# The front of a diffusion-transformer layer: who makes the low parts, in which order the first two projection blocks are multiplied, and when the masks are loaded

## The chip, the cores and the metric

The kernel runs on one core of a Trainium2 chip. The metric is the device time of one execution in microseconds, the median of several runs of the same program. Before the change it is 1540.49 us (three runs, 1539.71 to 1542.42). One execution was also recorded by the hardware profiler; all rows of the profile come from that one.

The core has five engines that run side by side, each with its own queue: TensorE (PE, matrix products; PEld is its weight load), VectorE (DVE), ScalarE (ACT), GpSimd (POOL), and SyncE (SP), which here only issues transfers. ScalarE issues a few transfers too.

## The reference

One layer of a hybrid backbone over 1024 latent tokens and 256 context tokens, width 1024, float32. Both kinds of token get their own adaLN vectors (shift and scale) from `SiLU(c) @ w_ada + b_ada`. What the front of the kernel computes is the first lines of this:

```python
mod_x = (jax.nn.silu(c) @ w_ada[i] + b_ada[i])[:, None, :]
mod_c = jax.nn.silu(c_ctx) @ w_ada[i] + b_ada[i]
px = modulate(rms_norm(x, norm1_w[i]), sh1, sc1) @ w_in[i]
pc = modulate(rms_norm(ctx, norm1_w[i]), csh1, csc1) @ w_in[i]
```

with `rms_norm(x, w) = x * rsqrt(mean(x*x) + eps) * w` and `modulate(h, shift, scale) = h * (1 + scale) + shift`. The columns of `w_in` feed a gated DeltaNet (short convolution, forward and backward scans) and a 2-D neighbourhood attention. Both results are concatenated and projected, and a SwiGLU feed-forward follows.

## The kernel before

**Layout.** Tokens lie along the free axis: 256 context tokens, then 1024 latent ones, 1280 in all. The width 1024 is cut into eight tiles of 128 partitions (`KT = 8`), called k below. A projection block is 128 output columns for all 1280 tokens; its sum over the eight tiles stands in three banks of the accumulation memory, for columns 0 to 256, 256 to 768 and 768 to 1280 (`SEGS`).

**Split products.** A float32 product is made of three faster ones. Every operand is split into a high part, rounded to the fast matmul type, and a low part, the rest. The terms are: 0, high weight by high tile; 1, high weight by low tile; 2, low weight by high tile. One term of one block and one tile is a group of three matmuls (256, 512 and 512 columns). The names are `whi`/`wlo` (from `fraw`) for the weights of the first two blocks, `zhi`/`zlo` for those of the third, and `hh[k]`/`hl[k]` for the tiles.

**The front, in program order** (lines 625 to 765):

1. The constants `cst` and the masks (256 KB) are loaded from ScalarE's queue. SP loads the eight x tiles, the raw weights of the first block, then eight 1 MB pieces of the adaLN weights (`wada`, seven buffers) with the raw weights of the second block among them. GpSimd casts the masks into `mr`, which is used far later.
2. `sums`: ScalarE squares each x tile, VectorE adds two of them, TensorE multiplies with a matrix of ones. This gives the sum of squares of each token, on all partitions. The first block's weights are split here: high part on ScalarE (line 216), low part on GpSimd (line 217).
3. ScalarE turns the sums into `rs`, the inverse root, by a logarithm and an exponential.
4. `ada(q)`, q = 0 to 3, yields the shift and scale of tiles 2q and 2q+1. It has two halves. In the first, eight products of `wada` leave a row, copied out of the bank by VectorE (q = 0, 1) or ScalarE. In the second, eight tiny products turn the row into columns (`pm<-sel,arow`), and VectorE makes `mod1` and `w1s` of them (lines 674, 675).
5. `normed(k)`: VectorE scales a tile in place by `w1s` and `rs` (line 695), first the 256 context columns, then the 1024 latent ones. ScalarE adds the shift and rounds: `hh[k]` (line 696). VectorE makes `hl[k]` (line 698).
6. `products(k, term, n)`: a group of three matmuls for tile k and block n.

`tile_pair` writes the order for tiles 0 and 1, 4 and 5, 6 and 7: terms 0 and 2 of both blocks for the first tile, then those of the second with the two halves of an `ada` between them, and term 1 of both tiles and blocks last. Tiles 2 and 3 are written out in the same manner. The second block's weights are split after `normed(0)`.

**What sets the order.** `pe.pinned` keeps TensorE in exactly the program's order in this stage. All other engines and SP's queue are put in order by a planner: it simulates the program with its own costs and gives each engine, among the instructions it holds to be ready, the one that comes first in the program. Every engine then works through its queue strictly in that order. Buffers are reused as soon as their last reader is done; the front's tiles give their room to later stages, the `wad` buffers of the second modulation (line 230) among them.

**What follows.** The two blocks are taken out of their banks (line 434), VectorE runs the convolution taps over them (line 443), and the other blocks, the scans, the attention and the feed-forward follow. Between the blocks, the second modulation (`modulation`, lines 220 to 257) sums 32 loads of 256 KB on VectorE; it must end (line 238 writes `modp`) before the accumulation banks are shared out anew, near 151 us.

Of the kernel before, what the change touches and what calls it, by code (L numbers as in the profile page):

```python
# [9 lines left out]
F32 = mybir.dt.float32  # L10
# [4 lines left out]
OP = mybir.AluOpType  # L15
# [4 lines left out]
D, L, CT, T = 1024, 1024, 256, 1280  # L20
KT = 8
# [66 lines left out]
def hybrid(ctx, tc, a, dbg):  # L88
    nc = tc.nc
    act, dve, pool, sp = nc.scalar, nc.vector, nc.gpsimd, nc.sync  # L90
# [45 lines left out]
    cst = const("cst", [128, NCONST])  # L136
# [64 lines left out]
            dve.scalar_tensor_tensor(r, y, 1.5, r, op0=OP.add, op1=OP.mult)  # L201

    def weights(wp, raws=2):
        def load(src, kt=KT, n=128, lo_engine=pool, raw=None, keep=None):
# [11 lines left out]
            act.copy(h, r)  # L216
            lo_engine.tensor_tensor(o, r, h.bitcast(F32), OP.subtract)
            return h, o
        return load

# [151 lines left out]
    with ExitStack() as bs:  # L372
# [31 lines left out]
        class Block:  # L404
# [7 lines left out]
            def prefetch(self, raw=None, keep=None):  # L412
# [3 lines left out]
                self.w = load_w(src, raw=raw, keep=keep)  # L416

            def banks(self):
                self.pss = [(bank("blk"), s0, n) for s0, n in self.segs]
# [206 lines left out]
        with ExitStack() as xs:  # L626
            xp = pools(xs, "xp", "left")
            xt = []
            act.dma_start(cst, a["cst"])
            masks = xp.tile([128, 4, 128], F32, name="masks", tag="masks")  # L630
            act.dma_start(masks, a["masks"])
            ascope = ExitStack()
            wap = pools(ascope, "wap", "right", 7)
            aw = {}
# [23 lines left out]
            def ada(q):  # L658

                p = bank("pm")  # L660
                for j in (2 * q, 2 * q + 1):
                    w = aw.pop(j)
                    for k in range(4):
                        pe.matmul(p[32 * k:32 * k + 32], wide[:, 4 * (j % 2) + k], w[:, k], start=j % 2 == 0,
                                  stop=j % 2 == 1)
                row = xp.tile([128, 512], F32, name="arow", tag="arow", bufs=2)
                (act.copy if q > 1 else dve.tensor_copy)(row, p)
                yield
                p = bank("pm")
                for b in range(4):  # L670
                    pe.matmul(p[:, 2 * b:2 * b + 2], row[:, b * 128:(b + 1) * 128], sel, start=True, stop=True)
                col = lambda x, b: x[:, b:b + 2].rearrange("p (b c) -> p b c", c=1).to_broadcast([128, 2, 2])
                for b0, s in ((8 + 2 * q, p[:, 0:4]), (2 * q, p[:, 4:8])):
                    dve.tensor_tensor(mod1[:, b0:b0 + 2], s.rearrange("p (b c) -> p b c", c=2), col(bada, b0), OP.add)
                dve.scalar_tensor_tensor(w1s[:, 2 * q:2 * q + 2], mod1[:, 8 + 2 * q:10 + 2 * q], 1.0, col(n1w, 2 * q),
                                         op0=OP.add, op1=OP.mult)
                yield

            def sums(ps, k):

                for k in (k, k + 1):
                    sq = xp.tile([128, T], F32, name="sq", tag="sq", bufs=4)
                    act.activation(sq, xt[k], AF.Square)
                    if k % 2 == 0:
                        even = sq
                dve.tensor_tensor(sq, sq, even, OP.add)
# [3 lines left out]
            def normed(k):  # L690

                t = xt[k]
                parts = [(1, slice(0, CT)), (0, slice(CT, T))]
                for j, x in parts:
                    dve.scalar_tensor_tensor(t[:, x], t[:, x], w1s[:, k, j:j + 1], rs[:, x], op0=OP.mult, op1=OP.mult)
                    act.activation(hh[k][:, x], t[:, x], AF.Identity, bias=mod1[:, k, j:j + 1])  # L696
                for j, x in parts:
# [12 lines left out]
            for k in (2, 4, 6):  # L710
                sums(ps, k)
            for p, (s0, n) in zip(ps, SEGS):
                act.activation(rs[:, s0:s0 + n], p[:, :n], AF.Ln, bias=b_eps, scale=1.0 / D)
# [10 lines left out]
            def tile_pair(k, nxt):  # L724

                if k:
                    normed(k)
                for term, n in (0, 0), (2, 0), (0, 1), (2, 1):
                    products(k, term, n)
                normed(k + 1)  # L730
                products(k + 1, 0, 0)
                products(k + 1, 0, 1)
                if nxt:
                    next(nxt)
                products(k + 1, 2, 0)
                if nxt:
                    next(nxt)
                products(k + 1, 2, 1)
                for i in (k, k + 1):
                    for n in range(2):  # L740
                        products(i, 1, n)

            tile_pair(0, adas[1])
            normed(2)
            products(2, 0, 0)
            products(2, 0, 1)
            next(adas[2])
            products(2, 2, 0)
            products(2, 2, 1)
            next(adas[2])  # L750
            normed(3)
            products(3, 0, 0)
            products(3, 0, 1)
            next(adas[3])
            products(3, 2, 0)
            next(adas[3])
            products(3, 2, 1)
            ascope.close()
            h_tiles(pools(bs, "hp2", "right"), 4)
            for i in (2, 3):  # L760
                for n in range(2):
                    products(i, 1, n)
            tile_pair(4, None)
            tile_pair(6, None)
            pe.pinned = False

        cp = pools(bs, "cp", "right")
# [584 lines left out]
    class Stream:  # L1352
# [430 lines left out]
```

## Time and profile before

| | us |
|---|---|
| median of three runs | 1540.49 |
| profiled execution, its own time | 1542.52 |
| its span in the trace | 1540.70 |
| TensorE busy | 1467.2 (95%) |
| VectorE busy | 1000.6 (65%) |
| ScalarE busy | 715.1 (46%) |
| GpSimd busy | 188.5 (12%) |

The span runs from the first to the last instruction of the record; the execution's own time is 1.82 us longer. Busy time of TensorE is modelled, since its products are pipelined: a TensorE that is busy may still run at a lowered clock, and the granted clock has a column of its own (1.00 is full speed, 0.50 is half). A row of the order of time has start, duration, engine, line, operation, output and inputs, shape and count; several instructions of one kind may be merged in it. Idle time in brackets is that of the engine ahead of the row, with what released it. A line can be that of a helper: L98 is every matmul.

### The profile page before, as it was taken

How to read it: one execution, taken by the hardware profiler on the slowest of the kernel's cores; microseconds unless marked ns; L12 is line 12 of the kernel's file. 1: busy time of each engine (PE TensorE's matmuls, PEld its weight loads, DVE VectorE, ACT ScalarE, POOL GpSimd, SP SyncE). 2: the span in 40 equal slices, each digit the busy share in tenths (PEclk: the TensorE clock that was granted, in tenths of full speed). 3: DMA queues.
4: the chain of work that ended last, by engine and by line, in shares of the span. 5: the costliest groups of instructions: out<-in, count | busy, mean ns of one | idle time of the engine just before them, and what ended most of it. 6: DMA issues, size and time to landing. Idle time of an engine off the chain costs nothing.

```text
span 1540.7 us, 23901 instructions
## 1 busy us (share of the span) xinstructions
PE 1467.2 (95%) x8553; PEld 1220.9 (79%) x8553; DVE 1000.6 (65%) x1911; ACT 715.1 (46%) x1396; POOL 188.5 (12%) x255
## 2 busy tenths in 40 slices
PE   4999998999999989998898989999999999999998
PEld 2789787778988868887787878888888888888887
DVE  4786579355255657678976489755565656689652
ACT  5343363684375355666643284333333334455441
POOL 1044610343143200000100000000000000000000
PEclk8999999899999999999999999999999999999999
DMA  9277133655477599997529404433332334798742
GB/s 367 95 227 247 47 90 117 234 145 190 151 247 241 157 275 287 276 261 217 171 78 324 149 35 136 147 106 104 105 106 99 106 101 156 237 378 293 235 154 82
DMA packets 208295, 276.30 MB, mean 179 GB/s; under 512 B 15968, under 2 KB 114864, under 8 KB 207152
## 3 DMA queue, kind: packets, MB, share of 16 engines
q1 hardware_dynamic: 207312, 274.15, 55.3%
q8 instruction: 67, 1.10, 0.3%
q10 hardware_dynamic: 864, 0.63, 0.1%
q14 instruction: 52, 0.43, 0.1%
HBM read 209.93 MB, written 68.98 MB: 181 GB/s over the span
## 4 chain that ended last, share of the span: by engine, by line
PE 49%; DVE 2%; ACT 1%; DMA 0%; issue 0%; SPq 0%; ACTq 0%; DVEq 0%
PE ps L98 46%; PE sc L98 2%; PE sc L102 1%; DMA wraw<-w_out 0%; DVE x L1541 0%; DVE bt L316 0%; ACT pt L329 0%; DVE lB L1535 0%; ACT x L1542 0%; DVE s L1227 0%; ACT L1445 0%; DVE bt L321 0%; DVE x L1454 0%; DVE oacc L1249 0%; DVE gal L1258 0%
## 5 line engine op out<-in xcount | busy, mean ns | idle before, releaser
L98 PE MATMUL ps<-hT,uhi 128*128 128x512 f32 x496 | 147.7, 392 | 3.2 <-ACT hT L1534 3.1
L98 PE MATMUL ps<-lT,uhi 128*128 128x512 f32 x496 | 146.7, 390 | 0.0
L98 PE MATMUL ps<-hT,ulo 128*128 128x512 f32 x496 | 146.7, 390 | 0.0
L98 PE MATMUL ps<-hB,uhi 128*128 128x512 f32 x436 | 129.7, 391 | 0.0
L98 PE MATMUL ps<-hB,ulo 128*128 128x512 f32 x436 | 129.3, 390 | 0.0
L98 PE MATMUL ps<-lB,uhi 128*128 128x512 f32 x436 | 129.3, 390 | 0.0
L1410 ACT CAST uhi<-ws 128x512 fp32r<-128x512 f32 x91 | 54.8, 623 | 149.9 <-PE ps L98 89.0
L1410 ACT CAST uhi<-wq 128x512 fp32r<-128x512 f32 x101 | 60.6, 621 | 136.5 <-PE ps L98 71.1
L98 PE MATMUL blk<-hh,whi 128*128 128x512 f32 (+1 forms) x392 | 117.5, 397 | 5.6 <-ACT hh L696 5.2
L1411 DVE TENSOR_TENSOR ulo<-wq,uhi 128x512 fp32r<-128x512 f32 x101 | 67.5, 687 | 69.2 <-ACT uhi L1410 37.5
L98 PEld LDWEIGHTS ps<-hT,uhi 128*128 128x128 f32 x496 | 93.4, 189 | 23.3 <-ACT hT L1534 3.5
L98 PE MATMUL blk<-hh,wlo 128*128 128x512 f32 (+1 forms) x392 | 109.2, 377 | 0.0
L98 PEld LDWEIGHTS ps<-hT,ulo 128*128 128x128 f32 x496 | 93.4, 188 | 19.6
L98 PEld LDWEIGHTS ps<-lT,uhi 128*128 128x128 f32 x496 | 93.4, 188 | 19.5
L98 PE MATMUL blk<-hl,whi 128*128 128x512 f32 (+1 forms) x392 | 106.9, 373 | 0.0
L98 PEld LDWEIGHTS ps<-hB,uhi 128*128 128x128 f32 x436 | 82.3, 189 | 17.5 <-issue 0.5
L98 PEld LDWEIGHTS ps<-hB,ulo 128*128 128x128 f32 x436 | 82.1, 188 | 17.2
L98 PEld LDWEIGHTS ps<-lB,uhi 128*128 128x128 f32 x436 | 82.1, 188 | 17.1
L98 PE MATMUL blk<-zhi,hh 128*128 128x264 f32 (+1 forms) x288 | 84.4, 293 | 1.6 <-DVE cacc L443 1.6
L1411 DVE TENSOR_TENSOR ulo<-ws,uhi 128x512 fp32r<-128x512 f32 x91 | 60.8, 686 | 36.8 <-ACT uhi L1410 28.5
L98 PE MATMUL blk<-zhi,hl 128*128 128x264 f32 (+1 forms) x288 | 81.7, 284 | 0.0
L98 PE MATMUL blk<-zlo,hh 128*128 128x264 f32 (+1 forms) x288 | 81.6, 283 | 0.0
(328 smaller groups left out, 3192.6 us busy)
## 6 DMA issues: line engine op xcount, KB each, us to landing
wq<-w_fo SPq DMA_DIRECT2D x99, 256.0 KB
wq<-w_gu SPq DMA_DIRECT2D x88, 256.0 KB
wad<-wa SPq DMA_DIRECT2D x64, 256.0 KB
bt<-rpb SPq DMA_DIRECT2D x64, 192.0 KB
t_d<-g SPq DMA_DIRECT2D x22, 512.0 KB
fr<-t_d SPq DMA_DIRECT2D x44, 256.0 KB
f_d<-g SPq DMA_DIRECT2D x33, 256.0 KB
fr<-f_d SPq DMA_DIRECT2D x33, 256.0 KB
```

Of the source, the lines that this page charges most:

```text
L98: i = nc.tensor.matmul(*args, **kw)
L102: i = nc.tensor.transpose(*args, **kw)
L1410: act.copy(hi, self.raw[key])
L1411: dve.tensor_tensor(lo, self.raw[key], hi.bitcast(F32), OP.subtract)
```

## The change

- The first block's low part (line 217) is made by VectorE instead of GpSimd, and its split is written behind all four `sums` instead of behind the first.
- The second block's high part is made before the first `ada`; its low part becomes a step `split` of its own on VectorE, behind the scaling of tiles 0 and 1.
- `normed(k)` is cut into `high(k)` (scaling and `hh`) and `low(k)` (`hl`). For tile 0, `high` works in three pieces of 256, 512 and 512 columns instead of two of 256 and 1024.
- The order of steps is written as one list, `plan`. In it `low` comes later than before, and term 1 of a tile comes behind the products of the next one.
- `warm(1)` is called twice: one 512-column product of constants into a bank that nobody reads, once behind the first half of `ada(0)` and once behind its second half.
- The masks' load moves from ScalarE's queue, ahead of the x tiles, to the end of the list of loads on SP; their tile is placed behind the x tiles.

```diff
-            act.dma_start(masks, a["masks"])
...
+            masks = xp.tile([128, 4, 128], F32, name="masks", tag="masks")
+            sp.dma_start(masks, a["masks"])
...
+            def cuts(k):
+                x = [(1, slice(0, CT)), (0, slice(CT, T))]
+                return x if k else x[:1] + [(0, slice(CT, CT + 512)), (0, slice(CT + 512, T))]
...
+            def warm(n):
+
+                p = bank()
+                for _ in range(n):
+                    pe.matmul(p, ident, cst[:, 0:512], start=True, stop=True)
...
-            sums(ps, 0)
-            first[0].prefetch(raws[0])
-            for k in (2, 4, 6):
+            for k in (0, 2, 4, 6):
                 sums(ps, k)
+            first[0].prefetch(raws[0], lo_engine=dve)
...
+            first[1].prefetch(raws[1], later=True)
             adas = [ada(q) for q in range(4)]
             next(adas[0])
+            warm(1)
             next(adas[0])
-            normed(0)
-            first[1].prefetch(raws[1])
+            warm(1)
             for b in first:
                 b.banks()
...
+            plan = [(high, 0), (high, 1), (split,), (products, 0, 0, 0), (products, 0, 2, 0), (products, 0, 0, 1),
+                    (low, 0), (products, 1, 0, 0), (products, 1, 2, 0), (products, 1, 0, 1), (1,), (low, 1),
+                    (products, 0, 2, 1), (1,), (high, 2), (products, 1, 2, 1), (high, 3), 0, 1, (products, 2, 0, 0), (products, 2, 0, 1), (2,),
+                    (low, 2), (products, 2, 2, 0), (products, 2, 2, 1), (2,), (products, 3, 0, 0), (products, 3, 0, 1), (3,),
+                    (low, 3), (products, 3, 2, 0), (3,), None, (high, 4), (products, 3, 2, 1), 2, 3]
+            for k in (4, 5, 6, 7):
+                if k > 4:
+                    plan.append((high, k))
+                plan += [(products, k, t, n) for t in (0, 2) for n in range(2)] + [(low, k)]
+                if k > 4:
+                    plan.append(k - 1)
+            plan.append(7)
```

In the list `(1,)` is the next half of `ada(1)`, a bare number is term 1 of that tile for both blocks, and `None` closes the adaLN weights' buffers and opens the tiles 4 to 7.

More of the change, by code (lines that the diff above doesn't have):

```diff
@@ L203, in weights, with load @@
     def weights(wp, raws=2):
-        def load(src, kt=KT, n=128, lo_engine=pool, raw=None, keep=None):
+        def load(src, kt=KT, n=128, lo_engine=pool, raw=None, keep=None, later=False):
             given = raw is not None
@@ L216, in load @@
             act.copy(h, r)
-            lo_engine.tensor_tensor(o, r, h.bitcast(F32), OP.subtract)
+            if not later:
+                lo_engine.tensor_tensor(o, r, h.bitcast(F32), OP.subtract)
             return h, o
@@ L410, in __init__, with prefetch @@
                 self.t0 = self.segs[0][0]
-            def prefetch(self, raw=None, keep=None):
+            def prefetch(self, raw=None, keep=None, **how):
                 i = self.i
@@ L415, in prefetch @@
                        "nq": lambda: a["w_nqk"][i], "nk": lambda: a["w_nqk"][4 + i]}[self.kind]()
[L416 removed]
+                self.w = load_w(src, raw=raw, keep=keep, **how)
             def banks(self):
@@ L629, in hybrid @@
             act.dma_start(cst, a["cst"])
-            masks = xp.tile([128, 4, 128], F32, name="masks", tag="masks")
-            act.dma_start(masks, a["masks"])
             ascope = ExitStack()
@@ L688, in sums, with high, low @@
                     pe.matmul(p[:, :n], M[C_ONE], sq[:, s0:s0 + n], start=k == 1, stop=k == KT - 1)
-            def normed(k):
+            def cuts(k):
+                x = [(1, slice(0, CT)), (0, slice(CT, T))]
+                return x if k else x[:1] + [(0, slice(CT, CT + 512)), (0, slice(CT + 512, T))]
+            def high(k):
                 t = xt[k]
-                parts = [(1, slice(0, CT)), (0, slice(CT, T))]
-                for j, x in parts:
+                for j, x in cuts(k):
                     dve.scalar_tensor_tensor(t[:, x], t[:, x], w1s[:, k, j:j + 1], rs[:, x], op0=OP.mult, op1=OP.mult)
                     act.activation(hh[k][:, x], t[:, x], AF.Identity, bias=mod1[:, k, j:j + 1])
-                for j, x in parts:
+            def low(k):
+                t = xt[k]
+                for j, x in cuts(1):
                     dve.scalar_tensor_tensor(hl[k][:, x], t[:, x], mod1[:, k, j:j + 1], hh[k][:, x].bitcast(F32),
@@ L715, in hybrid @@
                 act.activation(rs[:, x], rs[:, x], AF.Exp, scale=-0.5)
+            first[1].prefetch(raws[1], later=True)
             adas = [ada(q) for q in range(4)]
             next(adas[0])
+            warm(1)
             next(adas[0])
-            normed(0)
-            first[1].prefetch(raws[1])
+            warm(1)
             for b in first:
                 b.banks()
[L724 to L739, printed above, removed]
-                    for n in range(2):
-                        products(i, 1, n)
@@ L743, in hybrid @@
[L743 to L764, printed above, removed]
+            split = "split"
+            plan = [(high, 0), (high, 1), (split,), (products, 0, 0, 0), (products, 0, 2, 0), (products, 0, 0, 1),
[3 more added lines that the diff above has]
+                    (low, 3), (products, 3, 2, 0), (3,), None, (high, 4), (products, 3, 2, 1), 2, 3]
@@ new lines, in hybrid @@
+            for k in (4, 5, 6, 7):
[5 more added lines that the diff above has]
+            plan.append(7)
+            for step in plan:
+                if step is None:
+                    ascope.close()
+                    h_tiles(pools(bs, "hp2", "right"), 4)
+                elif isinstance(step, int):
+                    for n in range(2):
+                        products(step, 1, n)
+                elif step[0] is split:
+                    w = first[1].w
+                    dve.tensor_tensor(w[1], raws[1], w[0].bitcast(F32), OP.subtract)
+                elif len(step) == 1:
+                    next(adas[step[0]])
+                else:
+                    step[0](*step[1:])
```

## The prediction, made before the changed kernel was run

> **What bounds the kernel now.** I read the page first, then the list of what TensorE waited for, then the order of time from 13 to 76 us with its windows, because the diff touches only the front.
>
> ```profile
> span 1540.7 us, 23901 instructions
> PE 1467.2 (95%) x8553; PEld 1220.9 (79%) x8553; DVE 1000.6 (65%) x1911; ACT 715.1 (46%) x1396; POOL 188.5 (12%) x255
> PEclk8999999899999999999999999999999999999999
> ```
>
> TensorE is busy for 95% of the span, so a microsecond is saved where TensorE waits or runs at a lowered clock, and hardly anywhere else. The first digit of PEclk, 8, says that one such place lies in the first 38 us. The list of TensorE's waits (us in total, times, longest) names it:
>
> ```profile
> PE blk L98 <- ACT hh L696: 5.2, 3, 3.7
> PE m L98 <- DVE modp L238: 0.9, 1, 0.9
> ```
>
> The 3.7 us are the wait of the first block product for the first scaled tile. In order of time (start, duration; the bracket holds the idle time before and its releaser):
>
> ```profile
> 20.59 1.27 ACT L683 ACTIVATE sq<-xt 128x1280 f32<-128x1280 f32 x1 [0.31 <-DMA xt<-xcT]
> 26.81 0.16 PEld L98 LDWEIGHTS pm<-wada,wide 128*32 128x32 f32 x8 [0.86 <-DMA wada<-wa]
> 28.69 1.05 PE L98 MATMUL pm<-sel,arow 128*128 128x2 f32 x8 [0.81 <-DVE arow L667]
> 30.24 2.65 DVE L695 SCALAR_TENSOR_TENSOR xt<-xt,w1s,rs 128x256 f32<-128x256 f32 x1
> 30.27 2.34 POOL L217 TENSOR_TENSOR wlo<-fraw,whi 128x1024 fp32r<-128x1024 f32 x1 [4.67 <-ACT whi L216]
> 33.49 0.58 PE L98 MATMUL blk<-hh,whi 128*128 128x256 f32 x1 [3.75 <-ACT hh L696]
> 35.32 1.22 PE L98 MATMUL blk<-hh,whi 128*128 128x512 f32 x2 [1.25 <-ACT hh L696]
> 37.41 1.27 PE L98 MATMUL blk<-hh,whi 128*128 128x256 f32 x3
> 47.98 0.28 PE L98 MATMUL blk<-hh,whi 128*128 128x256 f32 x1
> 61.56 0.75 PE L98 MATMUL blk<-hh,whi 128*128 128x256 f32 x3
> 62.14 0.75 PE L98 MATMUL blk<-hh,wlo 128*128 128x256 f32 x3
> 75.63 0.51 PE L98 MATMUL blk<-hh,zhi 128*128 128x256 f32 x2
> ```
>
> Two things are to be seen. The VectorE scaling that starts at 30.24 lasts 2.65 us and ends 0.28 us after GpSimd's subtraction (30.27 + 2.34 = 32.61): it was held up for as long as GpSimd ran. And a group of three products lasts 1.27 us at 37.41, but 0.75 at 61.56, where the next one starts 0.58 us later. The clock shows why (window, its length, busy time of PE, PEld, DVE, ACT, POOL, then clock, DMA share, GB/s):
>
> ```profile
> 20.00:30.00 10.00, 7.90 (x36) 3.40 (x36) 2.63 (x6) 9.05 (x11) 2.68 (x1) 1.00 1.02 422
> 27.10:30.51 3.41, 1.83 (x16) 0.97 (x8) 1.32 (x5) 3.08 (x4) 0.24 (x1) 0.99 1.02 425
> 30.51:33.92 3.41, 0.43 (x1) 0.29 (x1) 3.41 (x2) 0.51 (x1) 2.10 (x1) 0.50 1.02 423
> 33.92:37.34 3.42, 2.17 (x6) 1.71 (x6) 3.42 (x6) 2.70 (x3) 0.00 (x0) 0.50 1.01 422
> 37.34:40.75 3.41, 3.41 (x11) 2.76 (x10) 1.52 (x2) 0.00 (x0) 0.00 (x0) 0.51 1.01 423
> 41.34:75.36 34.02, 33.75 (x198) 24.35 (x198) 25.28 (x38) 12.00 (x17) 2.55 (x1) 1.00 0.20 59
> 61.50:75.36 13.86, 13.86 (x72) 11.78 (x72) 11.37 (x13) 3.98 (x6) 2.55 (x1) 1.00 0.27 83
> 150.00:153.41 3.41, 2.12 (x17) 1.91 (x17) 2.21 (x5) 2.31 (x5) 1.07 (x1) 0.99 0.63 201
> 153.41:156.82 3.41, 3.41 (x12) 2.76 (x11) 3.31 (x7) 0.31 (x2) 3.26 (x5) 0.51 0.01 2
> 296.77:300.18 3.41, 1.78 (x9) 0.91 (x8) 0.82 (x2) 3.12 (x12) 2.15 (x7) 1.00 0.97 327
> ```
>
> From 30.5 to 40.7 us, three windows of 3.41 us, TensorE ran at half clock; one full window brought it back. I also see that transfers run flat out there (share 1.0, 422 GB/s), and that after 41 us TensorE is the bound (33.75 busy of 34.02).
>
> **The change, part by part.** Durations come from these groups (busy in all, mean ns, idle before) between 20 and 75.4 us, and from four rows of time:
>
> ```profile
> L695 DVE SCALAR_TENSOR_TENSOR xt<-xt,w1s,rs 128x1024 f32<-128x1024 f32 x8 | 10.2, 1279 | 0.0
> L251 DVE SCALAR_TENSOR_TENSOR acc<-wad,sc,acc 128x512 f32<-128x512 f32 x2 | 1.5, 752 | 0.1
> L686 DVE TENSOR_TENSOR sq<-sq 128x1280 f32<-128x1280 f32 x2 | 3.0, 1493 | 3.4 <-ACT sq L683 3.4
> L696 ACT ACTIVATE hh<-xt,mod 128x1024 fp32r<-128x1024 f32 x8 | 9.2, 1149 | 3.2 <-DVE xt L695 3.2
> L696 ACT ACTIVATE hh<-xt,mod 128x256 fp32r<-128x256 f32 x8 | 4.0, 501 | 15.2 <-DVE xt L695 15.2
> L713 ACT ACTIVATE rs<-m,bias 128x512 f32<-128x512 f32 x2 | 1.4, 688 | 0.6 <-PE m L98 0.6
> L98 PE MATMUL m<-sq,ones 128*128 128x512 f32 x8 | 3.8, 592 | 0.0
> masks<-masks ACTq DMA_DIRECT2D x1, 256.0 KB
> 13.33 0.61 POOL L655 CAST mr<-masks 128x512 fp32r<-128x512 f32 x1 [8.35 <-DMA masks<-masks]
> 41.34 1.92 PE L98 MATMUL pm<-wada,wide 128*32 128x512 f32 x16
> 43.20 0.85 PE L98 MATMUL blk<-hh,wlo 128*128 128x256 f32 x3
> 44.08 1.05 PE L98 MATMUL pm<-sel,arow 128*128 128x2 f32 x8
> 44.99 0.82 PE L98 MATMUL blk<-hh,wlo 128*128 128x256 f32 x3
> ```
>
> *Masks later.* Their 0.26 MB no longer travel among the eight x tiles, whose arrival paces the squares (20.59 waited for one). At 422 GB/s that is 0.62 us for everything that follows them, and the adaLN products at 26.81, which wait for their weights, follow them too: 0.62 us earlier. Below nothing this cannot go; if the masks had held nothing up, the gain is 0. The issue moves from ScalarE's queue to the end of SP's row of loads; the last of those loads waits for a buffer until 26.8, and the masks stand before or behind it. Behind them on SP is only the third block's weight load, needed near 68 us. Their cast (0.61 us of GpSimd) moves from 13.33, where VectorE had nothing to hold up, to when they land: some 40.5 us, behind half a weight block, five adaLN loads of 1 MB and themselves (6 MB at 422 GB/s, counted from 26.2). There it can block VectorE for 0 to 0.6 us; I take 0.5, since the third tile is then being scaled.
>
> *Low parts by VectorE.* Removed are two GpSimd subtractions of 2.3 to 2.7 us. A VectorE subtraction of 1024 columns is bounded by 1.19 (1493 x 1024/1280) and 1.28 (L695); I take 1.25. The first falls near 23 to 25 us, into VectorE's idle time before the row copy (costs nothing; uncovered it would cost 1.25). The second comes behind the scaling of both first tiles.
>
> *First tile in three pieces.* Before: transposed products end at 29.74, scaling starts 0.50 later. After: 29.74 - 0.62 + 0.04 (a product of constants ends just behind the row copy) = 29.16, scaling at 29.66. With 0.40 per 256-column piece, 0.75 per 512-column piece (L251) and 0.69 on ScalarE (L713 at 512; bounds 0.50 and 1.15 from L696), the high parts end at 30.64, 31.54 and 32.23. TensorE starts its three parts at 30.69, 31.59 and 32.28 and has done the first group at 32.5. Before, the second and third parts started at 35.32 and the group ended near 36.3, at half clock.
>
> *Two products of constants.* A 512-column float32 product takes two records of the m<-sq row, 0.43 us apart at best, 1.18 in sum at most: 0.86 to 1.2 us at full clock, twice that at half. The first lies in the 0.81 us while the row is copied, the second in the 1.5 us from 29.16 to 30.69. So about 0.04 us on the path; 0.4 if each takes 1.2.
>
> *Does the clock hold?* Between 29.1 and 32.5 TensorE would be busy for 0.86 + 0.11 + 0.22 + 0.22 = 1.4 us, a window shifted the other way holds 1.9 to 2.8. The rows: 1.78 busy of 3.41 held full clock at 296.77; 1.83 at 27.10 and 2.12 at 150.00 did not, but 1.05 of the first is two-column products. The new pauses hold real products, so I take that it holds.
>
> The Trainium skill, page "TensorE: Matmul & The Clock Gate", section "What's actually happening", gives a free-running window of 3413 ns and a fall after at least one idle window. Three windows in 10.2 us agree with the length; that the fall needs an idle window the trace does not bear out, for the window ahead of it was busy for 1.83 us. By the page's rule the clock surely holds; by the row it is rival B.
>
> *Low parts and products later.* The new order is written out, and TensorE keeps it. I walk it: w-low group and second block's group from 32.5 to 33.66; tile 1's high part is ready at 34.28 (scaling 31.42 to 33.09, 1.15 on ScalarE), a wait of 0.55; the second subtraction ends at 34.3, tile 0's low part at 35.8, tile 1's at 37.4, all before their products. First half of the second adaLN part at 35.94, one group at 37.80, then 0.23 of waiting for the row copy; both second low products and the four groups behind it fill 39.5 to 42.4. Tile 2 follows at 42.4 instead of 47.98.
>
> The sum for the whole stage, from the first product to 75.4 (just ahead of the third block's first products at 75.63): 48 groups of 13.86/24 = 0.578 are 27.7; three adaLN parts of 1.86 + 0.91 (41.34 to 43.20, 44.08 to 44.99) are 8.3; together 36.0. From 30.69 that is 66.7. Waits: first tile 1.2, tile 1 0.55, row copy 0.23 and again 0.2, tile 2 0.4, mask cast 0.5, tiles 4 to 7 0.8 (VectorE's work per tile, 11.37/4 = 2.8, is under TensorE's 3.5, but a tile's product order now asks for the next one earlier). That is 3.9: the stage ends at 70.6 instead of 75.4, 4.8 us earlier. I count 4.6, since every later engine works from TensorE's output and moves with it, but not to the last tenth. Bounds: with the first tile's wait alone 7.5; at half clock for two windows (rival B, 2.2) and with the masks gaining nothing, 1.8.
>
> The profiled execution took 1542.52 (span 1540.70 and 1.82 around it), 2.03 above the median of the runs, 1540.49. Its changed span would be 1536.1; from the median the forecast is 1540.5 - 4.6 = **1535.9 us**.
>
> **The rivals.** *B: the clock still falls in the front.* For it: two windows with 1.8 to 2.1 us of busy time fell. Against it: the pauses left are under 1 us. Two windows at half clock with some 4.5 us of products in them lose 2.2 us: 1538.1.
>
> *C: the gain is given back at the drain near 151 us.* There the second modulation must end before the banks are handed over, it is paced by its loads, and TensorE already waits 0.9 us on it. If these loads do not move up with the rest, up to the whole 4.6 is waited there; half to all leaves 1539.5. Against it: the loads are set off by VectorE's own steps and start earlier too.
>
> *D, slower: the lowered clock later on.* The stage's end moves by 4.6 us against windows of 3.41, so later pauses fall into other windows. A further window at half clock costs 1.7 us, as at 153.41. For it: 150.00 fell with 2.12 busy and 296.77 held with 1.78, so little decides. From three further windows on the kernel is not faster: 1540.5 - 4.6 + 3 or 4 x 1.7 = 1541 to 1542.7, say 1541.9. Against it: as many windows could be won.
>
> *E: the change does not do what it says,* since all but TensorE's order is set by the planner: were the second subtraction put ahead of the first scaling, TensorE would start 1.25 later: 1537.2, within the forecast's own range.
>
> **How the numbers follow.** Forecast with E 0.62 (own range 1533.5 to 1537.4), B 0.15, C 0.11, D 0.12. 0.2% is 3.1 us, what a measurement of this kernel can tell from no change; so faster means under 1537.4. Faster: 0.60 of the forecast, a third of B (0.05): 0.65. Slower: most of D, 0.10. Same: the rest, 0.25. The range from 1531.5 (the bound of 7.5 and most of a window at half clock won later on) to 1541.2 takes in B, C and half of D.
>
> **What would show it.** Right: no 2.6 us scaling, no GpSimd subtraction before 60 us, first block product near 30.7, clock 1.00 from 27 to 41 us, tile 2's first product near 42.4, third block near 70.6, and the same lead at 110, 200 and 1500 us. Wrong: half clock after 30 us (B); the lead gone between 126 and 160 us with longer waits on modp (C); the lead there at 110 us and lost in windows at 0.50 that are new (D); VectorE subtracting ahead of the first scaling (E).

## The result and the profile after

The changed kernel took **1536.21 us** (median of 10 runs, 1532.93 to 1538.45) where the kernel before took 1540.28 (10 runs): a ratio of 0.9971, with a 95% interval of 0.9961 to 0.9981. A second set of 11 runs gave 1538.21, a ratio of 0.9984 (0.9973 to 0.9994). Over all runs of this study the mean is 1537.2 (21 runs) against 1540.9 (106 runs), 3.6 us less; resampling the runs gives 2.7 to 4.6. The two sets of the changed kernel are themselves 2.0 us apart in the mean (1536.2 and 1538.2), though the program is the same, so differences of 2 us and less between kernels are not told from chance below, whatever the resampling of single runs says.

The page of the changed kernel's profiled execution (its own time 1532.93, the lowest of the 21):

```profile
span 1531.1 us, 23911 instructions
PE 1463.3 (96%) x8557; PEld 1217.1 (79%) x8557; DVE 1001.5 (65%) x1914; ACT 715.2 (47%) x1397; POOL 183.6 (12%) x253
PEclk9999999899999999999999999999999999999999
```

The first digit of PEclk has gone from 8 to 9. The list of TensorE's waits has 1.7 us on the scaled tiles, in five pieces, where 5.2 stood:

```profile
PE blk L98 <- ACT hh L700: 1.7, 5, 0.6
```

The same stage in order of time, and the clock in the windows quoted for before:

```profile
19.74 1.27 ACT L684 ACTIVATE sq<-xt 128x1280 f32<-128x1280 f32 x1 [0.33 <-DMA xt<-xcT]
22.45 1.22 DVE L218 TENSOR_TENSOR wlo<-fraw,whi 128x1024 fp32r<-128x1024 f32 x1
26.93 1.13 PE L98 MATMUL m<-cst 128*128 128x512 f32 x2
28.72 1.10 PE L98 MATMUL m<-cst 128*128 128x512 f32 x2
29.36 3.40 DVE L699 SCALAR_TENSOR_TENSOR xt<-xt,w1s,rs 128x256 f32<-128x256 f32 x5
30.44 0.38 PE L98 MATMUL blk<-hh,whi 128*128 128x256 f32 x1 [0.61 <-ACT hh L700]
31.32 0.50 PE L98 MATMUL blk<-hh,whi 128*128 128x512 f32 x1 [0.49 <-ACT hh L700]
31.98 0.50 PE L98 MATMUL blk<-hh,whi 128*128 128x512 f32 x1 [0.16 <-ACT hh L700]
32.68 1.22 DVE L759 TENSOR_TENSOR wlo<-fraw,whi 128x1024 fp32r<-128x1024 f32 x1
42.46 0.28 PE L98 MATMUL blk<-hh,whi 128*128 128x256 f32 x1
43.57 0.63 POOL L656 CAST mr<-masks 128x512 fp32r<-128x512 f32 x1 [38.60 <-DMA masks<-masks]
70.14 0.51 PE L98 MATMUL blk<-hh,zhi 128*128 128x256 f32 x2
```

```profile
27.10:30.51 3.41, 2.79 (x13) 1.38 (x13) 2.16 (x7) 2.75 (x4) 0.00 (x0) 1.00 1.02 423
30.51:33.92 3.41, 2.61 (x10) 1.59 (x10) 3.41 (x5) 2.91 (x4) 0.00 (x0) 1.00 1.02 423
```

The last square starts at 19.74 instead of 20.59, the five scalings of tiles 0 and 1 take 3.40 us instead of a first one of 2.65, and the first block product starts at 30.44 instead of 33.49. Tile 2 follows at 42.46 instead of 47.98, the third block at 70.14 instead of 75.63: a lead of 5.5 us. In this execution the clock stayed at 1.00 throughout.

The two profiled spans differ by 9.6 us, much more than the medians. From the third block on, the planner gave every engine the same order in both kernels, so the lead can be followed (shortest, median and longest duration in ns, then first and last start of a group; before and then after):

```profile
L891 ACT COPY N<-m x8: 575/582/587, 201.8 to 208.9; 80x512 f32<-80x512 f32 x8
L98 PE MATMUL sc<-pt,vw x384: 272/273/323, 566.5 to 794.5; 128*64 128x128 f32 x192
L98 PEld LDWEIGHTS ps<-hB,uhi x436: 187/188/330, 892.1 to 1535.8; 128*128 128x128 f32 x146
```

```profile
L890 ACT COPY N<-m x8: 575/582/587, 194.7 to 201.8; 80x512 f32<-80x512 f32 x8
L98 PE MATMUL sc<-pt,vw x384: 272/273/323, 560.2 to 788.7; 128*64 128x128 f32 x192
L98 PEld LDWEIGHTS ps<-hB,uhi x436: 187/188/330, 884.3 to 1526.2; 128*128 128x128 f32 x146
```

It is 5.5 us at 75, 7.1 at 202, 6.3 at 567, 5.8 at 794, 7.8 at 892 and 9.6 at the end. The two late steps up lie where before has a window of lowered clock that the changed kernel lacks (815 us), or a longer one (908); the step down after 202 us is the changed kernel's window at 293. The step near 151 us is of two kinds: before waits 0.9 us there for `modp`, which the changed kernel does not, and then loses a window. The step from 6.3 to 5.8 has no such window. After the front, before had 30.7 us at half clock, the changed kernel 20.5 (windows of before, then of the changed kernel; what lies in the last microseconds is left out):

```profile
153.35:156.77 3.42, 3.42 (x11) 2.81 (x11) 3.32 (x6) 0.26 (x2) 3.27 (x5) 0.50 0.01 2
269.41:279.65 10.24, 8.54 (x41) 7.48 (x42) 2.93 (x8) 3.41 (x8) 0.00 (x0) 0.50 0.40 142
559.54:566.37 6.83, 4.63 (x19) 3.31 (x18) 5.05 (x17) 4.32 (x10) 0.92 (x2) 0.50 0.89 258
815.54:818.95 3.41, 3.41 (x10) 2.65 (x9) 1.73 (x3) 1.33 (x3) 0.00 (x0) 0.50 1.05 349
907.70:914.53 6.83, 6.16 (x15) 4.81 (x16) 6.83 (x12) 6.80 (x12) 0.00 (x0) 0.50 0.10 38
```

```profile
262.30:272.50 10.20, 8.56 (x41) 7.48 (x42) 2.88 (x8) 3.41 (x8) 0.00 (x0) 0.50 0.41 143
293.02:296.44 3.42, 3.42 (x12) 2.58 (x12) 0.69 (x1) 2.85 (x9) 1.32 (x3) 0.50 0.84 221
555.82:559.24 3.42, 3.10 (x14) 2.35 (x14) 2.58 (x11) 1.61 (x3) 0.60 (x1) 0.50 0.82 213
900.58:904.00 3.42, 3.41 (x8) 2.73 (x9) 3.42 (x7) 3.41 (x5) 0.00 (x0) 0.50 0.00 0
```

10.2 us less at half clock and 4.1 us more lead (9.6 less 5.5) go together. That part is not the change's doing: where the windows lie differs from execution to execution of one kernel. Two later executions, one of each kernel, show what is left when the windows are alike. The second of before and the second of the changed kernel both had 37.5 us at half clock after the front; there the lead is 4.15 us at the third block (75.14 and 70.99), 4.5 at 892 and 4.6 at the end (before, then changed):

```profile
L98 PEld LDWEIGHTS ps<-hB,uhi x436: 187/188/330, 894.5 to 1537.6; 128*128 128x128 f32 x146
L98 PEld LDWEIGHTS ps<-hB,uhi x436: 187/188/329, 890.0 to 1533.0; 128*128 128x128 f32 x146
```

So the lead that the front gains is kept to the end.

### The profile page after: what moved, and what is told of

The parts are those of the page before. It is cut to its first block, busy times and chain, and to the rows that moved or that the text cites. A ratio compares the mean times of both kernels' runs of the same rounds, so it can differ in the third digit from the quotient of the medians.

```text
span 1531.1 us, 23911 instructions
## 1 busy us (share of the span) xinstructions
PE 1463.3 (96%) x8557; PEld 1217.1 (79%) x8557; DVE 1001.5 (65%) x1914; ACT 715.2 (47%) x1397; POOL 183.6 (12%) x253
## 4 chain that ended last, share of the span: by engine, by line
PE 48%; DVE 2%; ACT 1%; DMA 1%; issue 0%; SPq 0%; ACTq 0%; DVEq 0%
PE ps L98 46%; PE sc L98 2%; PE sc L102 1%; DMA wad<-wa 1%; DVE x L1540 0%; DVE bt L317 0%; DMA wq<-w_gu 0%; ACT pt L330 0%; DVE lB L1534 0%; ACT x L1541 0%; DVE s L1226 0%; ACT L1444 0%; DVE bt L322 0%; SPq L1381 0%; DVE x L1453 0%
## 5 line engine op out<-in xcount | busy, mean ns | idle before, releaser
L98 PEld LDWEIGHTS ps<-lB,uhi 128*128 128x128 f32 x436 | 82.1, 188 | 17.1
L1410 DVE TENSOR_TENSOR ulo<-ws,uhi 128x512 fp32r<-128x512 f32 x91 | 60.8, 687 | 37.6 <-ACT uhi L1409 29.3
```

The lines of the kernel that those rows point to most:

```text
L98: i = nc.tensor.matmul(*args, **kw)
L1410: dve.tensor_tensor(lo, self.raw[key], hi.bitcast(F32), OP.subtract)
```

## The experiments

For each run I read three things: the start of the third block's first products, the same counted from the last square (which takes out when the transfers brought the x tiles), and where the clock fell in the front.

| kernel | third block | after the last square | clock 0.50 in the front |
|---|---|---|---|
| before | 75.63 | 55.04 | 30.46 to 40.72 |
| before, second execution | 75.14 | 54.41 | 32.74 to 39.58 |
| before, third execution | 75.66 | 55.22 | 30.70 to 40.96 |
| before, low parts on VectorE | 73.13 | 52.38 | 30.28 to 37.12 |
| changed | 70.14 | 50.40 | none |
| changed, second execution | 70.99 | 50.92 | 31.42 to 34.84 |
| changed, products in a later pause | 71.29 | 51.14 | 31.90 to 35.31 |
| changed, products in a later pause and at the start | 71.12 | 51.29 | 31.75 to 35.16 |
| changed, no products of constants | 70.98 | 50.98 | 31.36 to 34.78 |
| changed, low parts on GpSimd | 73.63 | 53.91 | 34.18 to 37.54 |
| changed, first tile in two pieces | 72.65 | 51.64 | 32.98 to 36.40 |
| changed, masks first | 71.94 | 51.29 | 32.68 to 36.04 |
| changed, five products | 70.16 | 50.46 | none |
| changed, five products, second execution | 70.69 | 50.29 | none |

**Low parts back on GpSimd.**

```diff
-            first[0].prefetch(raws[0], lo_engine=dve)
+            first[0].prefetch(raws[0])
...
-            first[1].prefetch(raws[1], later=True)
+            first[1].prefetch(raws[1])
...
-            plan = [(high, 0), (high, 1), (split,), (products, 0, 0, 0), ...
+            plan = [(high, 0), (high, 1), (products, 0, 0, 0), ...
```

> The changed kernel with both low parts of the weights on GpSimd again. Theory (the held-up scaling was worth what it blocked): the first scaling is held up by 2.1 to 2.3 us again, the first block product starts near 32.7 instead of 30.4, the third block at 72.3 with the clock kept and at 74 with the clock lost; 2 to 4 us slower. Rival (VectorE's own 2.4 us for the two subtractions give the gain back): third block within 0.5 of 70.1, no change in time.

1540.92 us against 1540.04 of before, a ratio of 0.9997 (0.9983 to 1.0011); in the mean 3.4 us (1.6 to 5.1) over the changed kernel. In order of time:

```profile
29.36 2.67 DVE L699 SCALAR_TENSOR_TENSOR xt<-xt,w1s,rs 128x256 f32<-128x256 f32 x1
29.40 2.34 POOL L218 TENSOR_TENSOR wlo<-fraw,whi 128x1024 fp32r<-128x1024 f32 x1 [4.68 <-ACT whi L216]
32.62 0.38 PE L98 MATMUL blk<-hh,whi 128*128 128x256 f32 x1 [2.80 <-ACT hh L700]
```

The first scaling is held up again (2.67 instead of 0.5), TensorE starts 2.2 us later, the third block 3.5 us later. With everything else of the change in place, nothing is left of the gain.

**Low parts on VectorE, and nothing else.**

```diff
-            first[0].prefetch(raws[0])
+            first[0].prefetch(raws[0], lo_engine=dve)
...
-            first[1].prefetch(raws[1])
+            first[1].prefetch(raws[1], lo_engine=dve)
```

> The kernel before with the low parts of both first blocks on VectorE and nothing else changed (its order, its two pieces, its early masks). Theory (the held-up scaling is the largest term and stands alone): scaling at 30.2 lasts 0.5 us, the first block product starts at 31.3 instead of 33.5, the clock still falls in most executions since nothing fills the pause, the third block starts between 72.8 and 73.8 instead of 75.4, and the time is 1.8 to 2.5 us under that of before. Rival (it pays only with the later low parts, since VectorE's queue now holds the second subtraction ahead of tile 1's scaling): third block at 75 or later, no change in time.

1537.53 us against 1540.38, a ratio of 0.9987 (0.9973 to 1.0001). First block product at 31.47, third block at 73.13, 2.5 us earlier, with two windows at half clock. The theory's numbers for the trace are met, and the rival falls; the time gained, 2.9 us between the medians, is a little over the 1.8 to 2.5 expected. The interval of the time just reaches no change; its mean, 1537.9, lies 0.7 us (-1.1 to 2.6) over the changed kernel's, so what the other four edits add is too small to be told from nothing by time.

**No products of constants.**

```diff
             next(adas[0])
-            warm(1)
             next(adas[0])
-            warm(1)
```

> The changed kernel without its two products of constants. Theory (the products hold the clock): TensorE's clock falls to 0.50 between 29 and 34 us for two or three windows of 3.41 us, and the third block's first products start 2 to 3 us later than the changed kernel's 70.1 us; in all some 2 us slower. Rival (the pauses are already short enough once GpSimd is out of the way): the clock stays at 1.00, the third block starts at 70.1 +- 0.2, and the time is that of the changed kernel.

**The changed kernel once more.** The same program.

> The changed kernel once more. Theory (where the 3.41 us windows lie in an execution decides): if a window of this execution ends between 32.0 and 33.3 us, the clock is at 0.50 for one window from there and the third block starts 0.8 to 1.6 us later than 70.1; if not, the clock stays at 1.00 and it starts at 69.9 to 70.3. The time lies between 1532 and 1540 from execution to execution, with a median near 1536.2. Rival (the two products hold the clock in every execution): 1.00 throughout the front wherever the windows lie.

Without the products 1537.56 us, a ratio of 0.9981 (0.9969 to 0.9993); the mean is 0.1 us (-1.2 to 1.4) over the changed kernel's. The second execution of the changed kernel happened to have its windows at nearly the same place, which makes a clean pair. Windows of the changed kernel (second execution), then of the one without the products:

```profile
28.01:31.42 3.41, 2.39 (x12) 1.37 (x11) 2.22 (x7) 2.85 (x5) 0.00 (x0) 1.00 1.02 423
31.42:34.84 3.42, 3.33 (x8) 2.53 (x9) 3.42 (x5) 2.26 (x4) 0.00 (x0) 0.50 1.01 422
```

```profile
27.95:31.36 3.41, 1.42 (x9) 1.13 (x9) 2.23 (x7) 2.85 (x5) 0.00 (x0) 1.00 1.02 423
31.36:34.78 3.42, 3.34 (x8) 2.54 (x9) 3.42 (x5) 2.25 (x4) 0.00 (x0) 0.50 1.01 422
```

The products put another microsecond of work into the first window, and the clock fell all the same; the third blocks start at 70.99 and 70.98. So both theories were half wrong: the clock does fall without the products, but also with them, and for one window, not two or three. That window costs 0.5 us (50.92 against 50.40 after the last square), and 0.7 to 0.9 where it came later (51.14 with the products in a later pause, 51.29 with those at the start besides and with the masks first). In the seven executions of kernels with the changed front's order and VectorE's low parts, with two products or none, it fell in six; the first profile was the seventh.

It does not follow that the two products do nothing. The changed kernel's first execution and the kernel with GpSimd's low parts each had one window that took in both of them, whole in the first and most of them in the other, and there the clock held. That window of each, whole and then with the products of constants alone (PE, PEld, then idle engines):

```profile
26.76:30.17 3.41, 3.07 (x16) 1.49 (x12) 1.86 (x6) 2.86 (x5) 0.00 (x0) 1.00 1.02 423
26.76:30.17 3.41, 2.23 (x4) 0.60 (x4) 0.00 (x0) 0.00 (x0) 1.00 1.02 423
27.32:30.74 3.42, 2.51 (x12) 1.19 (x10) 2.17 (x5) 2.00 (x3) 1.34 (x1) 1.00 1.01 419
27.32:30.74 3.42, 1.83 (x4) 0.30 (x2) 0.00 (x0) 0.00 (x0) 1.00 1.01 419
```

The rest of the work in them is 0.97 us of two-column products and, in the first alone, some 0.2 us of others. In the second execution of the changed kernel, the window from 28.01 cuts the first product: 1.34 us of constants, 0.97 of two-column products. A count over the fourteen profiles fits this. Of 6025 windows at full clock between 20 and 1525 us, 85 were followed by half clock. Products of one or two columns left out, every window with under 1.5 us of modelled busy time was, and none with over 2.0 us; in between both happened, ten times with a fall. With the narrow products counted, windows of up to 2.6 us fell. The window from 28.01 has 1.7 us in this count, that without the products 0.4. So two products lift a window into the band where either can happen. This is a count, not an experiment: no run moved the windows at will.

**First tile in two pieces, and masks first.**

```diff
-                return x if k else x[:1] + [(0, slice(CT, CT + 512)), (0, slice(CT + 512, T))]
+                return x
```

> The changed kernel with the first tile scaled in two pieces. Theory (each piece sets its matmul free): the first group ends 0.4 to 0.5 us later and the third block starts at 70.5. Rival (the later wait for tile 1's high part takes it up): third block at 70.1, no change.

```diff
+            act.dma_start(masks, a["masks"])
...
-            sp.dma_start(masks, a["masks"])
```

> The changed kernel with the masks loaded from ScalarE's queue ahead of the x tiles again. Theory (0.26 MB at 422 GB/s stand ahead of the x tiles and the adaLN weights): the last square starts 0.6 to 0.85 us later (20.6 instead of 19.74) and the third block at 70.8 to 71.0; 0.6 to 0.9 us slower. Rival (the queues leave room for the masks): no shift.

Two pieces: 1539.13 us, a ratio of 0.9981 (0.9963 to 0.9999). Masks first: 1538.69, 0.9984 (0.9970 to 0.9998). Both intervals overlap with the changed kernel's own, so time does not separate them. The profiles say a little more. These two executions, and the one with products at the start, lost their window at nearly the same place, 11.9 to 12.0 us after the last square; two pieces need 51.64 after the last square, three need 51.29 in both others: 0.35 us for the third piece, near the 0.4 expected, from one execution against two. With the masks first the last square starts at 20.65, as before (20.59, 20.73, 20.44), against 19.7 to 20.4 with the masks late. But the two-piece kernel, with late masks, had it at 21.01, for another reason:

```profile
18.55 1.27 ACT L684 ACTIVATE sq<-xt 128x1280 f32<-128x1280 f32 x1 [0.32 <-DMA xt<-xcT]
21.01 1.27 ACT L684 ACTIVATE sq<-xt 128x1280 f32<-128x1280 f32 x1 [1.19 <-PE m L98]
```

The last square waited 1.19 us for TensorE to free a buffer. TensorE begins at half clock, and in that execution the trace's record of full clock starts only at 19.31 us, against 16.52 in the changed kernel's first. In the seven executions where it starts at 17.7 us or later the last square waited so, for 0.41 to 1.19 us; in the seven where it starts by 17.1 it did not. Among these seven the last square starts at 20.44 to 20.75 with early masks and at 19.70 to 19.83 with late ones: 0.6 to 1.05 us for the masks.

**Five products instead of two, twice.** One, two, and one ahead of each later third of the first group.

```diff
             next(adas[0])
-            warm(1)
+            warm(2)
             for b in first:
...
-                for o, s in b.outs:
+                for i, (o, s) in enumerate(b.outs):
+                    if i and (k, term, n) == (0, 0, 0):
+                        warm(1)
```

> The changed kernel with five products of constants instead of two: one, two, and one ahead of each of the two later thirds of the first group. Theory (the clock falls because the pauses are still too empty, not because products of constants do not count): with TensorE busy without a gap over 0.5 us from 27 to 34 us the clock stays at 1.00 wherever the windows lie, and the third block starts 50.2 to 50.6 us after the last square; the time is 0 to 1 us under that of the changed kernel. Rival (they do not count, or cost what they save): a window at 0.50 near 31 to 34 us as in the changed kernel's second profile, third block 51.0 to 51.6 after the last square, no gain.

> The changed kernel with five products of constants once more, since the windows of the execution profiled first ended at 30.0 and 33.4 us, where the changed kernel itself held the clock. Theory (products of constants hold the clock when they fill the pauses): with a window ending between 31.3 and 33.2 us the clock stays at 1.00 and the third block starts 50.2 to 50.6 us after the last square. Rival (they do not count): one window at 0.50, 51.0 to 51.6. In time the rival that they cost what they save: 1 to 2 us over the changed kernel's median of 1537.3, as in the run before.

1539.34 us, a ratio of 0.9989 (0.9978 to 0.9999), and 1539.28, 0.9992 (0.9981 to 1.0002). The clock held in both, and the third block came 50.46 and 50.29 after the last square. The first of the two says nothing: its windows ended 10.3 and 13.7 us after the last square, and in the changed kernel's first execution, which held as well, they ended at 10.4 and 13.9. The falls of the other kernels came at 11.35 to 12.03. The second execution had a window that ended at 12.1, next to the one of the kernel with masks first. Windows of that kernel, then of the one with five products:

```profile
29.27:32.68 3.41, 2.28 (x8) 0.94 (x8) 2.83 (x8) 2.78 (x5) 0.00 (x0) 1.00 1.01 423
32.68:36.09 3.41, 3.26 (x9) 2.78 (x10) 3.41 (x4) 1.65 (x3) 0.00 (x0) 0.50 1.02 423
```

```profile
29.07:32.48 3.41, 3.41 (x12) 1.81 (x13) 2.95 (x8) 2.85 (x5) 0.00 (x0) 1.00 1.02 423
32.48:35.89 3.41, 3.41 (x17) 2.54 (x16) 3.41 (x4) 1.53 (x2) 0.00 (x0) 1.00 1.02 423
```

There 2.28 us of work (2.0 without the two-column products) did not keep the clock, and 3.41 (3.2 without) did. So at this place more products of constants held it; one execution shows that. In time the two runs are 2.1 us (1.1 to 3.3) over the changed kernel, though the front ends as early and nothing behind it is ordered otherwise. Against the changed kernel's second set alone it is 1.2 us (-0.1 to 2.4), so that they are slower at all is not shown.

**Products of constants in a later pause, and at the start.** The fall from 262 to 273 us in the changed kernel's first profile, the longest there (10 us or more in every profile of a kernel with this chain), comes while TensorE waits for VectorE's elimination chain.

```diff
                     dve.tensor_tensor(N[:P, :, 0:c, c + 1:32], N[:P, :, 0:c, c + 1:32], t, OP.add)
+                    if 2 <= c <= 6:
+                        pe.matmul(bank(), N[:P, 0, c - 1:c + 3].rearrange("p r j -> p (r j)"), cst[:P, 0:512],
+                                  start=True, stop=True)
                     yield
```

> The changed kernel with five more products of constants near 260 us, each behind one of the last steps of VectorE's elimination chain (c from 6 to 2), where TensorE waits for 5.4 us and its clock falls in every profile seen so far. Theory (a lowered clock costs half the busy time of its windows): no 0.50 between 259 and 277 us, where 10.2 us stood, and 3.5 to 4.5 us faster than the changed kernel. Rival (the five products' 4.3 us and the order around them cost what the clock gives): within 1 us of the changed kernel.

1542.64 us, a ratio of 1.0016 (1.0004 to 1.0028): 5.7 us (4.3 to 7.2) slower than the changed kernel. Both theories missed. In order of time, and the window:

```profile
261.05 2.08 PE L98 MATMUL m<-cst,N 80*128 80x512 f32 x2 [5.16 <-DVE N L900]
272.28 0.17 DVE L906 MEMSET N<- 80x128 f32 x1 [5.98 <-PE m L98]
```

```profile
260.62:277.66 17.04, 16.61 (x40) 9.95 (x41) 5.50 (x12) 1.61 (x4) 0.00 (x0) 0.50 0.33 120
```

The first added product needs a step of the chain, so TensorE stands at it for 5.16 us, as it stood for 5.37 us at a later product in the changed kernel; the block products behind it wait too, the clock falls, the rest runs at half clock for 17 us, and the chain's last step now waits 5.98 us for the added products to read their operand. A product that depends on the late engine moves the pause and does not fill it.

```diff
             ps = [bank() for _ in SEGS]
+            p = bank()
+            for _ in range(4):
+                pe.matmul(p, ones, xt[0][:, CT:CT + 512], start=True, stop=True)
             for k in (0, 2, 4, 6):
```

> As the run before, and four products of ones and the first x tile ahead of the sums of squares, from 6.3 us on. Theory (TensorE starts at half clock and holds up the squares by up to 1.3 us in some executions): the sums of squares run at full clock from the first on, the last square never waits for TensorE, and the mean time is 0.3 to 0.8 us under that of the run before. Rival (the four products end after 12.8 us and push the sums back): third block 0.3 us later, no gain.

1543.83 us, 1.0020 (1.0008 to 1.0032), the kernel of the preceding run with four more products at the start. The sums of squares did run at full clock from the first (each took 2.42 us), the last square started at 19.83; the time shows no gain from it (0.8 us over the preceding run, with intervals that overlap).

**The kernel before, twice more.** The same program.

> The kernel before once more. Theory (the first profile of before showed a long fall, so part of the 5.5 us of lead at the third block is chance): the clock falls for one or two windows instead of three, and the third block starts at 74.2 to 75.0 us. Rival (before always loses three windows): 10.2 us at 0.50 from 30 us on and 75.4 again.

> The kernel before a third time, for the same question: third block at 74.2 to 75.0 with one or two windows at 0.50, or 75.4 with three.

Third block at 75.14 and 75.66, with 6.8 and 10.3 us at half clock: the first profile was typical of before. My theory that its front was unlucky has the number of windows right in one of two, and the third block's start (74.2 to 75.0) in neither. The second execution showed something else:

```profile
30.31 3.77 DVE L695 SCALAR_TENSOR_TENSOR xt<-xt,w1s,rs 128x256 f32<-128x256 f32 x2
30.40 2.60 POOL L217 TENSOR_TENSOR wlo<-fraw,whi 128x1024 fp32r<-128x1024 f32 x1 [4.68 <-ACT whi L216]
31.39 0.38 PE L98 MATMUL blk<-hh,whi 128*128 128x256 f32 x1 [1.58 <-ACT hh L696]
```

Here VectorE started 0.09 us ahead of GpSimd, did its small piece, and was held up in the large one (the two scalings took 3.77 us); in the first profile it started 0.03 us ahead and was held up at once.

## Why the prediction was right

The time, 1535.9 forecast and 1536.21 measured, and the sign were right. That the time agrees to 0.3 us is luck: the second set's median is 1538.21, and over all runs the gain is 3.6 us (2.7 to 4.6) where 4.6 was forecast. By its steps:

- **The held-up scaling** was the right cause, and the largest. First product forecast at 30.69, measured at 30.44; first group done at 32.5, measured 32.3; VectorE's subtractions 1.25, measured 1.22, the first in idle time. Undone alone it takes the whole gain back; done alone it brings 2.9 us in the mean (1540.9 to 1537.9).
- **The written-out order**: tile 2 at 42.4, measured 42.46; the stage 4.8 us earlier, measured 5.5, of which 0.5 is that this execution lost no window. Against the other executions of before and after in the table (75.14 and 75.66; 70.99) the lead is 4.15 to 4.7. From the first product the stage took 39.7 us, 39.9 forecast; among the waits, tiles 4 to 7 had 0.8 and lost 0.2 (24 groups from 56.06 to 70.14, 14.08 us against 13.86).
- **"I take that it holds"** is the step that failed. The clock held in the profile shown first, in the window that took in both products of constants (2.23 us of them); it fell in six of seven like executions, where the window took in one of them, or one and a piece of the other, or had none. The prediction took a window with 1.9 to 2.8 us of work for safe, from the row at 296.77 that held with 1.78; four windows starting between 28.0 and 29.3 held 2.3 to 2.4 us, 1.7 to 2.0 of it without the two-column products, and fell. Rival B happened in most executions, with the wrong price: one window, 0.5 to 0.9 us, not two and 2.2. By that size it changed little, which is why the sum came out right nevertheless. By the Trainium skill's page "TensorE: Matmul & The Clock Gate", section "What's actually happening", the clock falls after at least one idle window; so read, it would have held in the second execution too. The row 28.01:31.42, with 2.39 us of busy time ahead of a fall, decides against it here.
- **Masks**: 0.62 us forecast; the last square moved by 0.6 to 1.05 us where it did not wait for TensorE, whose slow start, up to 1.19 us of waiting, I had not counted. Their cast came at 43.57, not 40.5, held up a low part by 0.35 us (the four take 3.62 instead of 3.27), and no product waited for it: the 0.5 was not spent.
- **Rival C** fell: in the pair with like windows the lead was 4.15 us at the third block and 4.3 at 200 us (the copies `N<-m` start at 200.0 and 195.7). The wait for `modp` is in neither of these two; it comes and goes, 0.9 us in before's first execution and 1.0 in the changed kernel without products. **Rival D** named a real effect: the lead does step by some 2 us where windows differ. It has no preferred sign, and in the first pair it gave most of 4.1 us to the change instead of taking it.

What stays open: how much of the 3.6 us the order, the third piece and the late masks bring together. The profiles say some 0.85 us at the last square for the masks and 0.35 at the third block for the piece, with up to 0.9 for the luck of the windows beside them; the times do not resolve it.

## What to carry to other kernels

Where an instruction lasts a multiple of its own group's mean, look at what the other engine is doing in just that time; moving 2.4 us of work onto the very engine that was held up brought 2.9 of the 3.6 us in the mean. Before explaining the difference of two profiled executions, line them up and follow the lead: a step of some 2 us at one place can be a window of clock, and another execution of the same kernel may have it elsewhere. Run the same program in two sets before believing a difference of the size by which they differ. Work that is to fill a pause must not wait for what the pause waits for.

## What the runs showed of the hardware that was not expected

- All falls and rises of the clock in one execution lie on one grid of 3.413 us. In the first profile of before, the twelve edges from 30.46 to 914.5 leave remainders of 3.14 to 3.19 us; in the changed kernel's, eight edges leave 2.85 to 2.89. Other executions had 0.0, 0.7, 1.2, 1.8, 2.0 or 2.3: the grid's place is new in each, and the same program loses other windows each time.
- A microsecond at half clock after the front cost 0.35 to 0.6 us of time, by three pairs of executions: 17.1 us and 6.0 of lead (the changed kernel's two), 10.2 and 4.1 (the first pair, with the wait for `modp` in it), 6.8 and 4.0 (before's third against the changed kernel's second).
- Whether the clock is kept goes by the work in one window, and no window need be idle for a fall: in 6025 windows, all under 1.5 us of busy time fell and none over 2.0, products of one or two columns left out. Those seem hardly to count: the seven busiest windows that fell, 2.1 to 2.6 us, all had 0.3 to 1.05 us of them, as the one at 150.00 in before (2.12 us, 1.02 of it one-column products).
- TensorE begins at half clock though the granted clock reads 1.00: weight loads of 128 columns take 0.34 us at first and 0.19 later. The trace holds no record of the clock ahead of the change (16.4 to 19.3 us; 11.27 with products at the start), and the views count a stretch without a record as full. In seven executions this delayed the last square, by 0.41 to 1.19 us.
- Of two engines that meet within 0.1 us, the one that the trace shows first is not always the one that goes first: VectorE was 0.02 to 0.04 us ahead of GpSimd and held up in three executions, 0.09 us ahead and not in a fourth.
